# Transposing the heads' outputs by VectorE blocks and moves between partition quarters, instead of by TensorE

## The chip, the core and the metric

The kernel runs on one core of a Trainium2 chip. The metric is the device time of one execution in microseconds, as the median of several runs. A core has TensorE (PE, the matmuls, with its weight loads as PEld), VectorE (DVE), ScalarE (ACT), GpSimd (POOL), SyncE (SP, which here only issues DMAs) and 16 DMA engines. A tile lies in 128 partitions; a "quarter" is 32 of them. TensorE's output goes to PSUM banks of 512 fp32 per partition and is read from there by ACT or DVE ("evicted").

## The reference

One decoder block, 512 tokens, model width 1024, everything fp32. Two branches share the projections of the normed input, a gated short convolution and a four-head mLSTM (256 wide in q and k, 512 in v):

```python
hn = rmsnorm(x, g_mix[l])
proj = jnp.einsum('bsd,de->bse', hn, w_in[l])
(xa, ba, ca, za, q, k, v, o, zb, ig, fg, ga, gb) = jnp.split(proj, SPLIT_POINTS, axis=-1)
ya = ba * causal_short_conv(ca * xa, conv_w[l], conv_b[l])
ya = jnp.einsum('bsc,cd->bsd', ya * jax.nn.silu(za), w_a_out[l])
...
hb = mlstm_chunkwise(q..., k..., v..., ig, fg)          # per head: decayed scores @ v / max(|n.q|, 1)
hb = rmsnorm(hb, g_head[l].reshape(N_HEADS, DV)).reshape(bsz, s, V_DIM).astype(x.dtype)
yb = jax.nn.sigmoid(o) * hb * jax.nn.silu(zb)
yb = jnp.einsum('bsv,vd->bsd', yb, w_b_out[l])
merged = jax.nn.sigmoid(ga) * ya + jax.nn.sigmoid(gb) * yb
x = x + jnp.einsum('bsd,de->bse', merged, w_o[l])
... # a gated per-layer embedding is added, then a last rmsnorm
```

The edit concerns `yb`: each head leaves it as tokens x values (512 x 512), and the product with `w_b_out` needs values x tokens. `g_head` is a factor per value, so it can be applied before or after the transpose, or later.

## The kernel before, in words

**Products.** Each fp32 matmul is three matmuls of a rounded format (`mm3`, L233 to L235): high x high, low x high, high x low. So every weight is split: ACT writes the high part (`whi`, L180), DVE the rest (`wlo`, L181), in halves of 128x1024, shortly before use. The large projections are Strassen products (`strassen`, L318 to L387): seven products (0 to 6) of two steps each, and the weights' sums that they need are made by accumulating DMAs on POOL's queue (`add_chunk`, L156: a second weight block is added in DRAM-to-SBUF transfers onto `wraw`). Plain weight loads are issued by SP (L148).

**Order.** PE, ACT, DVE and POOL work strictly in the order in which the program writes its instructions. `step` (L223) ends each half product: it calls `tick` (L216), which starts fresh tasks (evictions), then emits one half of a weight split, then one piece of every active generator (heads' scores, transposes, loads). A generator that yields 16 times therefore lasts 16 half products, each 2.7 us or more of TensorE. Within a Strassen product the eviction `v` (`snap`, L346, ACT) reads the bank of product 2; product 3 adds into that same bank, so TensorE waits for `v` there.

**Stages** (us in the profiled execution): head 0's v and o (74 to 112), weighted sum `pv` (to 118), z for heads 0 and 1 (to 157), merge gates (to 196), head 1's v and o (to 239), pv (to 246), head 2's q and k (to 288), v and o (to 330), pv (to 337), z for heads 2 and 3 (to 375), gates (to 415), head 3's v and o (to 458), pv (to 465), the convolution's four Strassen products (465 to 628), the convolution's output product (to 666), then `w_b_out`.

**Heads.** `head` fills `vv` (v, high and low; ACT L929, DVE L932) and the normed, gated output `y` (tile `gty`). `turn` (L799) then transposes it: 8 groups of 8 PE transposes of 128x128 (L810), 16 evictions by ACT that apply `g_head` (`gh`, L805) into `yc`, and one DMA of 1 MB on POOL's queue to `yt_d` in DRAM (L813). It is started two or three ticks after the head. The tiles `vv`, `yc` and `qk_raw` (the next head's q and k, loaded by SP at L825) share one buffer in turn (tag "vv"), as does later one half of the convolution's result `ya` (L410). At 628 us the four `yt_d` are loaded again as `yf`, and `left_first` makes the Strassen sums and splits of them.

Of the kernel before, what the change touches and what calls it, by code (L numbers as in the profile page):

```python
# [22 lines left out]
DV = 512  # L23
# [6 lines left out]
HC = 4  # L30
# [6 lines left out]
def hybrid_block(ctx, tc, x, p, g_mix, w_in, conv_w, conv_b, w_a_out, b_gates, g_head,  # L37
                 w_b_out, w_o, g_ple, w_ple_gate, w_ple, g_final, out):
    nc = tc.nc
    act, dve, pool, pe = nc.scalar, nc.vector, nc.gpsimd, nc.tensor  # L40
# [7 lines left out]
    ps_x = ctx.enter_context(tc.tile_pool(name="ps_x", bufs=4, space=bass.MemoryType.PSUM))  # L48
# [21 lines left out]
    H2 = S // 2  # L70
# [47 lines left out]
    spare = {b12[0]: None}  # L118
# [22 lines left out]
    raws, splits, pieces, active, fresh = {}, {}, deque(), [], []  # L141
# [111 lines left out]
    ident = const.tile([P, P], F32, name="ident")  # L253
# [14 lines left out]
    yt_d = [dram.tile([P, 2, HC, H2], F32, name=f"yt_d{h}") for h in range(NH)]  # L268
# [255 lines left out]
    gh = prm[:, 40:56]  # L524
# [48 lines left out]
    def quarter(q):  # L573
        hi, lo = (u[:, q % HH, :] for u in splits[0][q // HH])
        return hi, lo, raws[0][:, q, :]
# [6 lines left out]
    hi, lo, raw = quarter(0)  # L582
# [59 lines left out]
    for g in range(2):  # L642
        src = wg_raw[:, :, g * NH:(g + 1) * NH]
# [57 lines left out]
    B = nc.vector.STREAM_SQUARE_SIZE  # L701
# [94 lines left out]
        a = POFF[j] + (t - j) * P  # L796
        return u[:, a:a + P]

    def turn(h, y):  # L799

        yc = hp.tile([P, 2, 2, HC, H2], F32, name="yc", tag="vv", align_bytes=256)[:, 0]
        pts = {}
        for i in range(3):
            for v in range(2 * i - 2, 2 * i) if i else ():
                act.activation(yc[:, :, v, :], pts[v].rearrange("p (h s) -> p h s", h=2), AF.Copy,  # L805
                               scale=gh[:, 4 * h + v:4 * h + v + 1])
            for v in range(2 * i, 2 * i + 2) if i < 2 else ():
                pts[v] = ps_x.tile([P, S], F32, name="pty", tag="x")
                for t in range(NT):
                    pe.transpose(pts[v][:, t * P:(t + 1) * P], y[:, t, v * P:(v + 1) * P], ident)  # L810
            if i < 2:
                yield
        nc.gpsimd.dma_start(yt_d[h], yc)  # L813

    def qk_tile():
        both = hp.tile([P, 2, 4, S], F32R, name="qk", tag="qk", align_bytes=256)
        return [both[:, i] for i in range(2)]

    def recut(h, qk):

        for _ in range(7):
            yield
        raw = hp.tile([P, 2, 4, S], F32, name="qk_raw", tag="vv", align_bytes=256)[:, 0]
        for m in range(4):
            nc.sync.dma_start(raw[:, m, :], qk_d[h][:, m, :])  # L825
        yield
        yield
        yield
        qk.extend(qk_tile())
        for m in range(4):  # L830
            cut(qk[0][:, m, :], qk[1][:, m, :], raw[:, m, :])
            if m < 3:
                yield
# [69 lines left out]
    def head(h, qk):  # L903
        vv = []

        def sink_qk(n, t, src):

            fs, ps = slice(2 * (t % 2), 2 * (t % 2) + 2), slice(t // 2 * H2, (t // 2 + 1) * H2)
            src = src.rearrange("p (f s) -> p f s", f=2)
            if n == 1:  # L910
                nc.gpsimd.dma_start(qk_d[h + 1][:, fs, ps], src)
                return
            if not qk:
                qk.extend(qk_tile())
            cut(*[u[:, fs, ps] for u in qk], src)
            yield

        if h == 2:
            strassen(hn_lhs, sink_qk, True)
        pr = [hq2.tile([P, 1280], F32R, name=f"pr{i}", align_bytes=256) for i in range(2)]  # L920
        pp = hq2.tile([P, 1280], F32, name="pp")
        gt = []

        def sink_vo(n, t, src):
            if n == 0:
                if not vv:
                    both = hp.tile([P, 2, NT, DV], F32R, name="vv", tag="vv", align_bytes=256)
                    vv.extend(both[:, i] for i in range(2))
                act.activation(vv[0][:, t, :], src, AF.Copy)  # L929
                if t < 2:  # L930
                    yield
                dve.tensor_tensor(vv[1][:, t, :], src, vv[0][:, t, :].bitcast(F32), ALU.subtract)  # L932
            elif h % 2:
                so = temp("e", "so")
                act.activation(so, src, AF.Sigmoid)
                dve.tensor_tensor(gt[0][:, t, :], gt[0][:, t, :], so, ALU.mult)
            else:
                act.activation(gt[0][:, t, :], src, AF.Sigmoid)
            yield

        def scored():
            both = hp.tile([P, 2, NT, DV], F32, name="gty", tag="qk", align_bytes=256)
            gt.extend(both[:, i] for i in range(2))
            if h % 2:
                nc.gpsimd.dma_start(gt[0], z_d[h])

        active.append(scores(h, qk, pr, pp, scored))
        strassen(hn_lhs, sink_vo)
        gt, y = gt

        def weighted_sum(t, ps):
            dve.tensor_scalar(y[:, t, :], ps, inv[:, t:t + 1], None, ALU.mult)
            junk = temp("e", "junk")
# [24 lines left out]
        def sink_z(n, t, src):  # L978
            sz = temp("e", "sz")
            act.activation(sz, src, AF.Sigmoid)  # L980
            if n == 1:
                dve.tensor_tensor(src, sz, src, ALU.mult)
                nc.gpsimd.dma_start(z_d[h + 1][:, t, :], src)
                yield
                return
            dve.tensor_tensor(sz, sz, src, ALU.mult)
            dve.tensor_tensor(gt[:, t, :], gt[:, t, :], sz, ALU.mult)
            yield
            norm(t)
            yield  # L990

        active.append(rsqrt())
        if h % 2 == 0:
            strassen(hn_lhs, sink_z)
        return y

    def finish(h, y, wait):
        for _ in range(wait):
            yield
        yield from turn(h, y)  # L1000

    hp_ctx, hp = open_pool("heads")
    hq_ctx, hq2 = open_pool("scores")
    load_maxima(0)
    qks = [qk_tile()] + [[] for _ in range(3)]
    for h in range(NH):
        y = head(h, qks[h])
        active.append(finish(h, y, 2 + h % 2))
        if h % 2 == 0:
            active.append(recut(h + 1, qks[h + 1]))  # L1010
            strassen(hn_lhs, sink_gate(h))
    close(hq_ctx)

# [15 lines left out]
    yf = {h: (wbp if h == 3 else yfp).tile([P, 2, HC, H2], F32, name=f"yf{h}", tag=f"yf{h}", align_bytes=256) for h in (0, 2, 1, 3)}  # L1029
# [6 lines left out]
    def left_high(k):  # L1036
# [7 lines left out]
        act.activation(units[k][0], src, AF.Copy, scale=scale)  # L1044
        return lambda: dve.scalar_tensor_tensor(both[:, 1], src, scale, both[:, 0].bitcast(F32), ALU.mult, ALU.subtract)

    def left_first():
        for _ in range(5):
            yield
        for k in range(3):  # L1050
            low = left_high(k)
            yield
            low()
            yield
        for g in range(2):
            (a11, a21), (a12, a22) = ([yf[2 * g + r][:, v] for v in range(2)] for r in range(2))
            dve.tensor_tensor(hsf[g], a22, a21, ALU.subtract)
            yield
            dve.tensor_tensor(a21, a11, a21, ALU.subtract)
            yield  # L1060
            dve.tensor_tensor(a11, hsf[g], a11, ALU.add)
            yield
            if g == 0:
                dve.tensor_tensor(a12, a11, a12, ALU.subtract)
                yield
# [18 lines left out]
    todo = deque((n, t) for n, ts in ((0, (0, 1)), (1, range(NT)), (0, (2, 3))) for t in ts)  # L1084
# [140 lines left out]
    half = [slice(0, CW), slice(CW, D)]  # L1225
# [177 lines left out]
    q = [slice(CW, CW + CW // 2), slice(CW + CW // 2, D)]  # L1403
# [50 lines left out]
```

## Time and profile before

| | before |
|---|---|
| runs, median (lowest to highest) | 845.53 us (845.30 to 846.86) |
| the profiled execution, its span | 847.37 us, 845.6 us |
| PE busy | 834.5 us, 4584 instructions |
| DVE, ACT, POOL busy | 651.0, 495.5, 210.0 us |
| granted clock of PE | 0.998 |
| DMA | 173.89 MB, 206 GB/s over the span |
| `yt_d<-yc` put, 1 MB, x4 | 4.9 us from issue to landing (median) |

"Busy" is the time in which an engine executes. An engine's wait is put down to what ended it. A DMA's "landing" is the time from its issue until its last byte is written. Off the path of the busiest engine a wait costs nothing by itself.

### The profile page before, as it was taken

Reading aid. Unit: us, or ns where it says so; the run is one execution under the profiler, and the core shown is the slowest. Engines: PE = TensorE matmul, PEld = TensorE weight load, DVE = VectorE, ACT = ScalarE, POOL = GpSimd, SP = SyncE. Lnnn points to the kernel's source line nnn. Section 1 sums busy time; section 2 is a strip of 40 time slices with the busy share of each in tenths; the row PEclk is TensorE's granted clock in tenths of the full one; section 3 lists DMA queues with packets and bytes.
Section 4 is the critical chain, followed back from the end, with each engine's and each line's share of the span. In section 5 each row is a group of like instructions: output and inputs, shape, how many; then the busy total and the mean of one; then the engine's idle time right before and its main releaser. Section 6 shows DMA issues by size and latency. Waiting matters only on the chain.

```text
span 845.6 us, 12113 instructions
## 1 busy us (share of the span) xinstructions
PE 834.5 (99%) x4584; PEld 726.7 (86%) x4584; DVE 651.0 (77%) x878; ACT 495.5 (59%) x720; POOL 210.0 (25%) x203
## 2 busy tenths in 40 slices
PE   8999999999999999999999999999999999999996
PEld 7888888887889988888788999999998888888885
DVE  5788767975787677788668779897986677999565
ACT  6467665666865566665776654555453256667543
POOL 5203122203124321220222333433411122131031
PEclk9999999999999999999999999999999999999999
DMA  9748779779978997896898799899989488999402
GB/s 310 269 145 183 159 166 220 194 274 227 252 159 207 244 225 180 199 215 199 258 243 211 156 218 169 194 184 182 181 255 380 101 194 214 284 258 229 187 0 100
DMA packets 103939, 173.89 MB, mean 206 GB/s; under 512 B 5632, under 2 KB 46132, under 8 KB 102600
## 3 DMA queue, kind: packets, MB, share of 16 engines
q0 software_dynamic: 39488, 70.33, 44.6%
q1 hardware_dynamic: 59792, 94.64, 33.7%
q10 hardware_dynamic: 4600, 8.14, 3.1%
q8 instruction: 36, 0.59, 0.3%
q14 instruction: 23, 0.19, 0.1%
HBM read 156.30 MB, written 16.79 MB: 205 GB/s over the span
## 4 chain that ended last, share of the span: by engine, by line
PE 92%; DMA 3%; DVE 2%; issue 1%; ACT 1%; SPq 0%; POOL 0%; POOLq 0%; ACTq 0%; DVEq 0%
PE mm L234 28%; PE mm L235 28%; PE mm L233 28%; PE pv L233 1%; PE pv L235 1%; PE pv L234 1%; DMA wraw<-in_w_ple 1%; DMA wraw<-in_w_b_out 1%; PE pty L810 1%; DMA sg_d<-c 1%; PE sc L235 1%; PE sc L234 1%; PE sc L233 1%; DVE wlo L181 1%; PE ptk L1247 0%
## 5 line engine op out<-in xcount | busy, mean ns | idle before, releaser
L181 DVE TENSOR_TENSOR wlo<-wraw,whi 128x1024 fp32r<-128x1024 f32 x244 | 299.4, 1229 | 104.7 <-ACT whi L180 98.8
L180 ACT ACTIVATE whi<-wraw 128x1024 fp32r<-128x1024 f32 x246 | 257.1, 1054 | 103.8 <-PE mm L235 48.8
L156 POOL DMA_DIRECT2D wraw<-in_w_in x112 | 136.9, 1423 | 335.4 <-DVE wlo L181 207.7
L346 ACT ACTIVATE s<-mm 128x512 f32<-128x512 f32 x84 | 50.2, 597 | 100.2 <-PE mm L235 98.7
L233 PE MATMUL mm<-whi,hs 128*128 128x512 f32 x256 | 99.9, 390 | 0.0
L234 PE MATMUL mm<-wlo,hs 128*128 128x512 f32 x256 | 99.8, 390 | 0.0
L235 PE MATMUL mm<-whi,hs 128*128 128x512 f32 x256 | 99.7, 389 | 0.0
L233 PE MATMUL mm<-hn_hi,whi 128*128 128x256 f32 (+1 forms) x304 | 93.3, 307 | 0.0
L235 PE MATMUL mm<-hn_hi,wlo 128*128 128x256 f32 (+1 forms) x304 | 92.9, 306 | 0.0
L234 PE MATMUL mm<-hn_lo,whi 128*128 128x256 f32 (+1 forms) x304 | 92.8, 305 | 0.0
L233 PE MATMUL mm<-hs,whi 128*128 128x256 f32 x320 | 90.9, 284 | 0.0
L234 PE MATMUL mm<-hs,whi 128*128 128x256 f32 x320 | 90.5, 283 | 0.0
L235 PE MATMUL mm<-hs,wlo 128*128 128x256 f32 x320 | 90.5, 283 | 0.0
L234 PE MATMUL mm<-wlo,hn_hi 128*128 128x512 f32 x192 | 75.3, 392 | 0.4 <-DVE wlo L181 0.2
L233 PE MATMUL mm<-whi,hn_hi 128*128 128x512 f32 x192 | 74.9, 390 | 0.0
L235 PE MATMUL mm<-whi,hn_lo 128*128 128x512 f32 x192 | 74.8, 389 | 0.0
L234 PEld LDWEIGHTS mm<-hs,whi 128*128 128x128 f32 x320 | 61.4, 192 | 0.0
L233 PEld LDWEIGHTS mm<-hs,whi 128*128 128x128 f32 x320 | 61.4, 192 | 0.0
L235 PEld LDWEIGHTS mm<-hs,wlo 128*128 128x128 f32 x320 | 61.4, 192 | 0.0
L235 PEld LDWEIGHTS mm<-hn_hi,wlo 128*128 128x128 f32 x304 | 58.1, 191 | 2.5
L234 PEld LDWEIGHTS mm<-hn_lo,whi 128*128 128x128 f32 x304 | 58.1, 191 | 2.4
L233 PEld LDWEIGHTS mm<-hn_hi,whi 128*128 128x128 f32 x304 | 58.1, 191 | 2.4
(339 smaller groups left out, 1670.2 us busy)
## 6 DMA issues: line engine op xcount, KB each, us to landing
wraw<-in_w_in SPq DMA_DIRECT2D x32, 1024.0 KB, 6.1
wraw<-in_w_in POOLq DMA_DIRECT2D x52, 512.0 KB, 8.5
wraw<-in_w_in SPq DMA_DIRECT2D x48, 512.0 KB, 5.6
wraw<-in_w_in POOLq DMA_DIRECT2D x60, 256.0 KB, 5.7
wraw<-in_w_b_out SPq DMA_DIRECT2D x7, 1024.0 KB, 7.0
wraw<-in_w_b_out POOLq DMA_DIRECT2D x12, 512.0 KB, 7.0
wraw<-in_w_o SPq DMA_DIRECT2D x5, 1024.0 KB, 7.4
yt_d<-yc POOLq DMA_DIRECT2D x4, 1024.0 KB, 4.9
```

What stands on the lines that cost most here:

```text
L156: nc.gpsimd.dma_start(raws[to][:, ks, cs], src[:, ks, :], accum_op=ALU.add)
L180: act.activation(hi, t, AF.Copy)
L181: (e_lo or dve).tensor_tensor(lo, t, hi.bitcast(F32), ALU.subtract)
L233: pe.matmul(ps, lhsT=a[0], rhs=b[0], start=first, stop=False, **kw)
L234: pe.matmul(ps, lhsT=a[0], rhs=b[1], start=False, stop=False, **kw)
L235: pe.matmul(ps, lhsT=a[1], rhs=b[0], start=False, stop=last, **kw)
L346: act.activation(to[i], src, AF.Copy, scale=scale)
L810: pe.transpose(pts[v][:, t * P:(t + 1) * P], y[:, t, v * P:(v + 1) * P], ident)
```

## The change: what it does

- The PE transposes and their evictions go. `turning(h, half)` gives three functions: `turn(y, t)` transposes 32x32 blocks of a 128x512 tile on DVE (one instruction), `move(i, on_dve)` copies one of 16 combinations of a source quarter and a destination quarter (32 partitions) on DVE or ACT, `put(i)` sends a part to `yt_d`.
- Even heads work in two halves of two tiles each (2 x 16 moves of 256 elements, a put of 512 KB after each); odd heads in one go (16 moves of 512 elements, then two puts of 512 KB, in pieces of 1 KB). Heads 0 and 2 give ACT 22 moves and DVE 10, head 1 eight each, head 3 eleven and five.
- The steps are spread over 16 ticks by plans of (ACT moves, DVE moves) per tick, so that the last put of heads 0 and 2 comes in the next odd head's v and o stage, that of head 1 in head 2's, and that of head 3 in the convolution.
- `qk_raw` is no tile of its own: it takes the other half of the even head's `yc`, and is loaded by SP earlier.
- The first two tiles of an even head are transposed one tick after their norm in z's sink; `sink_qk` waits four ticks before its first two cuts.
- `g_head` is applied to the loaded `yf` by 16 ACT operations of 128x512 in `left_first` (`scale_head`).

```diff
-    def turn(h, y):
-        yc = hp.tile([P, 2, 2, HC, H2], F32, name="yc", tag="vv", align_bytes=256)[:, 0]
...
-                act.activation(yc[:, :, v, :], pts[v].rearrange("p (h s) -> p h s", h=2), AF.Copy,
-                               scale=gh[:, 4 * h + v:4 * h + v + 1])
...
-                    pe.transpose(pts[v][:, t * P:(t + 1) * P], y[:, t, v * P:(v + 1) * P], ident)
...
-        nc.gpsimd.dma_start(yt_d[h], yc)
+    def turning(h, half):
+        both = hp.tile([P, 2, NT, DV], F32, name="yc", tag="vv", align_bytes=256)
+        spare, blocks, spread = both[:, 0], both[:, 0], both[:, 1].rearrange("p t v -> p (t v)")
+        n = NT
+        if half:
+            n = NT // 2
+            blocks, spread = both[:, 1, :n], both[:, 1, n:].rearrange("p t v -> p (t v)")
+        spread = spread.rearrange("p (v s) -> p v s", v=HC)
+        def turn(y, t):
+            dve.transpose(blocks[:, t % n, :], y[:, t, :])
+        def move(i, on_dve):
+            b, q = divmod(i, P // B)
+            src = blocks[b * B:(b + 1) * B].rearrange("p t (v q a) -> p t v q a", q=P // B, a=B)[:, :, :, q]
+            dst = spread[q * B:(q + 1) * B].rearrange("p v (t b a) -> p t v b a", t=n, a=B)[:, :, :, b]
+            if on_dve:
+                dve.tensor_copy(dst, src)
+            else:
+                act.activation(dst, src, AF.Copy)
+        def put(i):
+            nc.gpsimd.dma_start(yt_d[h][:, i], spread if half else spread[:, :, i * H2:(i + 1) * H2])
...
+    def finish(h, y, tools):
+        turn, move, put, _ = tools or turning(h, False)
+        if h % 2 == 0:
+            yield from moves(move, [(2, 0), (2, 0), (3, 0), (3, 0), (2, 0), (1, 0), (2, 0), (1, 0)])
+            put(0)
+            for t in (2, 3):
+                turn(y, t)
                 yield
+            yield from moves(move, [(0, 1), (0, 1), (1, 3), (1, 1), (2, 2), (2, 2)])
+            put(1)
+            return
+        for _ in range(4):
+            yield
+        for ts in ((0,), (1,), (2,), (3,)) if h == 1 else ((0, 1), (), (2,), (3,)):
+            for t in ts:
+                turn(y, t)
+            yield
+        yield from moves(move, [(1, 1)] * 8 if h == 1 else [(3, 0), (3, 1), (2, 1), (1, 1), (2, 2)])
+        for i in range(2):
+            put(i)
...
-        raw = hp.tile([P, 2, 4, S], F32, name="qk_raw", tag="vv", align_bytes=256)[:, 0]
...
+            for _ in range(4 if t < 2 else 0):
+                yield
...
+    def scale_head(h):
+        for v in range(HC):
+            act.activation(yf[h][:, :, v, :], yf[h][:, :, v, :], AF.Copy, scale=gh[:, HC * h + v:HC * h + v + 1])
     def left_first():
         for _ in range(5):
             yield
+        for h in (0, 2):
+            scale_head(h)
+            yield
         for k in range(3):
             low = left_high(k)
             yield
             low()
-            yield
+            if k:
+                scale_head(2 * k - 1)
+                yield
```

Three places in the order of instructions follow. A row is line, operation, output<-input and the output's shape; in brackets are the semaphores that it waits for: an engine's name stands for that engine, DMASW for the landing of a DMA issued by POOL, DMAHW for one issued by SP or ACT.

POOL, from the end of head 0's gate stage into head 1's v and o stage, before (`wraw` are the accumulating weight loads, `yt_d` the put of the head's output):

```order
L983 DMA z_d_100<-c 128x512 [waits DVE_49]
L813 DMA yt_d_90<-yc 128x2048 [waits DMASW1_49,Activation_49]
L156 DMA wraw_1609<-in_w_in 128x2x512 [waits DMAHW4_49,DMAHW7_49,DMASW2_49,DVE_49]
L156 DMA wraw_1609<-in_w_in 128x2x512 [waits DMASW3_49,DVE_49]
L156 DMA wraw_1692<-in_w_in 128x2x512 [waits DMAHW1_49,DMAHW0_49,DMASW4_49]
L156 DMA wraw_1692<-in_w_in 128x2x512 [waits DMASW5_49]
L156 DMA wraw_1609<-in_w_in 128x2x512 [waits DMASW6_49,DMASW2_49,DVE_49]
L156 DMA wraw_1609<-in_w_in 128x2x512 [waits DMASW7_49,DMASW3_49,DVE_49]
```

The same place now:

```order
L822 DMA yt_d_90<-yc 128x1024 [waits DMASW1_49,Activation_49]
L156 DMA wraw_1598<-in_w_in 128x2x512 [waits DMAHW3_49,DMAHW7_49,DMASW2_49,DVE_49]
L156 DMA wraw_1598<-in_w_in 128x2x512 [waits DMASW3_49,DVE_49]
L156 DMA wraw_1686<-in_w_in 128x2x512 [waits DMAHW4_49,DMAHW1_49,DMASW4_49]
L156 DMA wraw_1686<-in_w_in 128x2x512 [waits DMASW5_49]
L156 DMA wraw_1598<-in_w_in 128x2x512 [waits DMASW6_49,DMASW2_49,DVE_49]
L822 DMA yt_d_90<-yc 128x1024 [waits DMASW7_49]
L156 DMA wraw_1598<-in_w_in 128x2x512 [waits DMASW3_49,DMASW0_49,DVE_49]
```

The put of 2048 elements ahead of all the loads is now two of 1024, and the second stands behind the fifth load.

ACT, in the first half of head 1's v and o stage, before (`e` are the exponentials of the scores, `vv` the new head's v, `v` the Strassen eviction, `whi` the weight split):

```order
L872 ACTIVATE e<-mxb,colsb 128x128 x2
L929 ACTIVATE vv<-c 128x512 [waits DMASW1_49]
L346 ACTIVATE v<-mm 128x512 [waits PE_49]
L180 ACTIVATE whi_1943<-wraw_1739 128x1024 [waits Activation_49]
L872 ACTIVATE e<-mxd,colsb 128x128 [waits DVE_49,Activation_49]
```

Now:

```order
L916 ACTIVATE e<-mxb,colsb 128x128 x2
L975 ACTIVATE vv<-c 128x512 [waits DMASW7_49,Activation_49]
L346 ACTIVATE v<-mm 128x512 [waits PE_49]
L180 ACTIVATE whi_1955<-wraw_1735 128x1024
L916 ACTIVATE e<-mxd,colsb 128x128 [waits DVE_49,Activation_49]
```

The order around it is the same; `vv` waited for the landing of the one put (DMASW1), and now waits for that of the second put (DMASW7) and for the moves.

DVE, about 45 us into the convolution, before and then now (`ya` is the convolution's result, in the buffer that held head 3's `yc`):

```order
L410 TENSOR_TENSOR ya_4712<-cv,ya_4711 128x2x256 [waits DMASW4_49]
L447 TENSOR_TENSOR m<-m,cz 128x512
L181 TENSOR_TENSOR wlo_4778<-wraw_4434,whi_4777 128x1024 [waits Activation_49]
L399 TENSOR_SCALAR cv<-cu,prm 128x256 [waits DVE_49]
L401 SCALAR_TENSOR_TENSOR cv<-cu,prm,cv 128x256 [waits DVE_49] x2
```

```order
L181 TENSOR_TENSOR wlo_4722<-wraw_4292,whi_4721 128x1024 [waits PE_49,Activation_49]
L445 TENSOR_TENSOR m<-c 128x512 [waits DVE_49]
L455 COPY cu<-cu 128x2x2
L456 TENSOR_TENSOR cu<-m,mm 128x2x256 [waits DVE_49,PE_49]
L181 TENSOR_TENSOR wlo_4763<-wraw_4435,whi_4762 128x1024 [waits DMAHW2_49,DMAHW1_49,Activation_49]
L410 TENSOR_TENSOR ya_4730<-cv,ya_4729 128x2x256 [waits DMASW7_49,DMASW0_49]
L447 TENSOR_TENSOR m<-m,cz 128x512
L181 TENSOR_TENSOR wlo_4796<-wraw_4435,whi_4795 128x1024 [waits Activation_49]
```

`ya` waited for one put, and now for both of head 3's; a weight split stands right behind it. On POOL these two puts stand behind the first four 256 KB loads of `wraw_4292` (weights of the convolution).

More of the change, by code (lines that the diff above doesn't have):

```diff
@@ L797, in ptile @@
         return u[:, a:a + P]
-    def turn(h, y):
-        yc = hp.tile([P, 2, 2, HC, H2], F32, name="yc", tag="vv", align_bytes=256)[:, 0]
[L802 to L805, printed above, removed]
-                               scale=gh[:, 4 * h + v:4 * h + v + 1])
[L807 to L811, printed above, removed]
-                yield
-        nc.gpsimd.dma_start(yt_d[h], yc)
+    def turning(h, half):
[18 more added lines that the diff above has]
+            nc.gpsimd.dma_start(yt_d[h][:, i], spread if half else spread[:, :, i * H2:(i + 1) * H2])
+        return turn, move, put, spare
@@ new lines, in moves @@
+    def moves(move, plan):
+        todo = deque(range((P // B) ** 2))
+        for n_act, n_dve in plan:
+            for i in range(max(n_act, n_dve)):
+                if i < n_act:
+                    move(todo.popleft(), False)
+                if i < n_dve:
+                    move(todo.popleft(), True)
+            yield
+        assert not todo
+    def finish(h, y, tools):
[5 more added lines that the diff above has]
+                turn(y, t)
+                yield
+            yield from moves(move, [(0, 1), (0, 1), (1, 3), (1, 1), (2, 2), (2, 2)])
[10 more added lines that the diff above has]
+            put(i)
@@ L817, in qk_tile, with recut @@
         return [both[:, i] for i in range(2)]
-    def recut(h, qk):
+    def recut(h, raw, qk):
         for _ in range(7):
             yield
-        raw = hp.tile([P, 2, 4, S], F32, name="qk_raw", tag="vv", align_bytes=256)[:, 0]
         for m in range(4):
@@ L990, in sink_z @@
             yield
+            if t < 2:
+                yield
+                if not tools:
+                    tools.extend(turning(h, True))
+                tools[0](y, t)
+                yield
+        tools = []
         active.append(rsqrt())
@@ L994, in head @@
             strassen(hn_lhs, sink_z)
-        return y
-    def finish(h, y, wait):
-        for _ in range(wait):
-            yield
-        yield from turn(h, y)
+        return y, tools
     hp_ctx, hp = open_pool("heads")
@@ L1006, in hybrid_block @@
     for h in range(NH):
-        y = head(h, qks[h])
-        active.append(finish(h, y, 2 + h % 2))
+        y, tools = head(h, qks[h])
+        active.append(finish(h, y, tools))
         if h % 2 == 0:
-            active.append(recut(h + 1, qks[h + 1]))
+            active.append(recut(h + 1, tools[3], qks[h + 1]))
             strassen(hn_lhs, sink_gate(h))
@@ L1045, in left_high @@
         return lambda: dve.scalar_tensor_tensor(both[:, 1], src, scale, both[:, 0].bitcast(F32), ALU.mult, ALU.subtract)
+    def scale_head(h):
+        for v in range(HC):
+            act.activation(yf[h][:, :, v, :], yf[h][:, :, v, :], AF.Copy, scale=gh[:, HC * h + v:HC * h + v + 1])
     def left_first():
         for _ in range(5):
+            yield
+        for h in (0, 2):
+            scale_head(h)
             yield
@@ L1053, in left_first @@
             low()
-            yield
+            if k:
+                scale_head(2 * k - 1)
+                yield
         for g in range(2):
```

## The prediction

> **What bounds the kernel now.** I read the page's busy times and its chain first, then the groups of the tile that the change removes, then the stages by windows, the waits, and last the timeline at the places where the order of instructions changes.
>
> ```profile
> PE 834.5 (99%) x4584; PEld 726.7 (86%) x4584; DVE 651.0 (77%) x878; ACT 495.5 (59%) x720; POOL 210.0 (25%) x203
> PE 92%; DMA 3%; DVE 2%; issue 1%; ACT 1%; SPq 0%; POOL 0%; POOLq 0%; ACTq 0%; DVEq 0%
> ```
>
> TensorE is busy for 834.5 of 845.6 us and is 92% of the chain that ended last. So the time is a stream of matmuls with hardly a hole in it: whatever leaves TensorE is gained in full, whatever runs on another engine is free until a matmul has to wait for it, and from there on it costs in full.
>
> ```profile
> L810 PE MATMUL pty<-ident,gty x64: 270/272/273, 164.7 to 480.8; 128*128 128x128 f32 x64
> L805 ACT ACTIVATE yc<-pty,prm x16: 672/682/692, 166.5 to 482.3; 128x512 f32<-128x512 f32 x16
> ...
> 164.90 0.87 PE pty L810 x8
> ```
>
> The 64 transposes are 8 groups of 8. A group holds the chain of waits for 0.87 us.
>
> **The change: what it removes.** 8 groups × 0.87 us = 7.0 us leave TensorE, all of it on the path, since nothing else fills TensorE's time there. The 16 evictions on ScalarE (16 × 0.68 = 10.9 us) ran beside matmuls; their loss is worth nothing by itself.
>
> **What it adds on VectorE and ScalarE.** No row of this profile shows a move between partition quarters of this size, so I take bounds.
>
> ```profile
> L891 DVE STREAM_TRANSPOSE pp<-pp 128x512 f32<-128x512 f32 x4 | 2.8, 706 | 0.0
> L895 DVE COPY pp<-pp 32x16 f32<-32x16 f32 x12 | 2.0, 164 | 0.2
> L399 DVE TENSOR_SCALAR cv<-cu,prm 128x256 f32<-128x256 f32 x16 | 6.2, 385 | 0.0
> ...
> L240 ACT ACTIVATE qk<-qk_raw 128x512 fp32r<-128x512 f32 x8 | 4.9, 619 | 0.0
> L875 ACT ACTIVATE pr<-pp 128x256 fp32r<-128x256 f32 x4 | 1.6, 410 | 0.7 <-DVE pp L880 0.6
> ```
>
> A block transpose is 16 × 0.71 = 11.3 us in all. A move of 256 elements is between 0.16 (the small copy L895) and 0.39 us (L399) on VectorE, and I take 0.39, since L399 has its length; on ScalarE 0.41 (L875). A move of 512 is taken at 0.7 on VectorE (as L891, the same length) and 0.62 on ScalarE (L240). Heads 0 and 2: 22 moves on ScalarE = 9.0 us and 10 on VectorE = 3.9 us each. Head 1: 8 × 0.62 = 5.0 and 8 × 0.7 = 5.6. Head 3: 11 × 0.62 = 6.8 and 5 × 0.7 = 3.5. The 16 g_head scalings (128x512, 0.62) are 9.9 us of ScalarE. VectorE gains 28 us, ScalarE 29 net of the evictions. What counts is where.
>
> ```profile
> 185.80:200.70 14.90, 14.81 (x64) 11.66 (x63) 9.62 (x13) 12.48 (x20) 3.13 (x4) 1.00 0.80 246
> 196.00:239.00 43.00, 42.91 (x194) 34.94 (x193) 31.36 (x51) 31.05 (x48) 10.29 (x9) 1.00 1.02 249
> 628.00:666.00 38.00, 38.00 (x169) 31.43 (x169) 25.54 (x33) 11.36 (x12) 6.04 (x10) 1.00 0.83 302
> ```
>
> The columns are the stretch, its length, then busy us of PE, PEld, DVE, ACT and POOL, the granted clock, the DMA share and GB/s. The scalings fall in 628 to 666, where ScalarE is busy 11.4 of 38 us: 9.9 more fit, cost 0; without that cover each would delay a weight split by 0.6. The tight place is the end of a gate stage (185.8 to 200.7): ScalarE has 2.4 us free, and the moves of the even head sit between the splits there. About 0.9 us per even head would reach TensorE (two or three VectorE moves of 0.39 ahead of one wlo); but the next stall, below, is pinned to a DMA that started before, and takes this delay in. I count 0 for it, and up to 2 × 0.9 = 1.8 as a bound. Transposes and the other moves fit beside: VectorE has 43.0 − 31.4 = 11.6 us free in 196 to 239.
>
> **The moved puts: the term that decides.** Before, each head's output left as one 1 MB put (L813) shortly after the head, long ahead of its buffer's next use. Now the last put of a head stands 16 or 17 ticks later, in the next odd stage for heads 0 and 2. In POOL's order it comes right behind the fifth accumulating weight load (L156, `wraw`) of that stage. The tile `vv` of the next head takes the same buffer, so ScalarE's first `vv` (L929, L975 in the new kernel) waits for the put's landing. Behind it in ScalarE's queue stands the eviction `v` (L346), which empties the bank that the fourth Strassen product adds into; TensorE waits for that, and for the half operand split (`whi`, L180, `wlo`, L181) behind it.
>
> How long do these loads take to land? First the four loads of 197.1 to 200.3, then the fifth:
>
> ```profile
> L156 POOL DMA_DIRECT2D wraw<-in_w_in x4: 1227/1465/2199, 197.1 to 200.3; - x4
> ...
> DMA to landing us min/median/max: 7.7/10.9/14.9
> L156 POOL DMA_DIRECT2D wraw<-in_w_in x1: 1194/1194/1194, 207.5 to 207.5; - x1
> ...
> DMA to landing us min/median/max: 11.2/11.2/11.2
> ```
>
> The first lands at 204.8, the fourth at 200.3 + 14.9 = 215.2, the fifth at 207.5 + 11.2 = 218.7: one 512 KB load each 3.5 us, in the order of issue (the five take 13.9 us from the first landing to the last), with a DMA share of 1.02 in this stage. So a put issued behind the fifth cannot overtake it. What it takes beyond is shown by a plain 1 MB transfer behind such a load:
>
> ```profile
> gty<-z_d POOLq DMA_DIRECT2D x1, 1024.0 KB, 7.7
> wraw<-in_w_in POOLq DMA_DIRECT2D x1, 512.0 KB, 6.0
> ```
>
> The load was issued at 224.2 and landed at 230.2, gty at 225.1 and 232.8: 2.6 us later for 1 MB, so 1.3 us for a 512 KB put.
>
> The row of issues and landings says: strictly in order. [...] Were the put free of the loads ahead, the waits below would be near 0 and the sum a gain (the first rival). The trace goes against it in every one of these landings.
>
> Stall A (head 0's put, head 1's vv):
>
> ```profile
> 214.36 0.62 ACT L929 ACTIVATE vv<-c 128x512 fp32r<-128x512 f32 x1
> 214.88 0.58 ACT L346 ACTIVATE v<-mm 128x512 f32<-128x512 f32 x1
> 215.36 1.05 ACT L180 ACTIVATE whi<-wraw 128x1024 fp32r<-128x1024 f32 x1
> ...
> 216.44 1.23 DVE L181 TENSOR_TENSOR wlo<-wraw,whi 128x1024 fp32r<-128x1024 f32 x1 [1.00 <-ACT whi L180]
> 216.62 0.40 PE L233 MATMUL mm<-whi,hs 128*128 128x512 f32 x1
> ```
>
> The put lands at 218.7 + 1.3 = 220.0; vv and v then end at about 221.05 (0.52 from start to start, 0.58 for v). TensorE wanted the bank at 216.62: 4.4 us. Then whi and wlo end at 223.3, against 221.05 + 6 matmuls of 0.23 = 222.4 when the second half is wanted: 0.9 more. A = 5.3 us.
>
> Stalls B (head 1's two puts, head 2's vv) and C (head 2's, head 3's):
>
> ```profile
> L156 POOL DMA_DIRECT2D wraw<-in_w_in x1: 1197/1197/1197, 297.0 to 297.0; - x1
> ...
> DMA to landing us min/median/max: 10.3/10.3/10.3
> 302.16 0.62 ACT L929 ACTIVATE vv<-c 128x512 fp32r<-128x512 f32 x1
> 307.76 0.40 PE L233 MATMUL mm<-whi,hs 128*128 128x512 f32 x1
> L156 POOL DMA_DIRECT2D wraw<-in_w_in x1: 1194/1194/1194, 426.2 to 426.2; - x1
> ...
> DMA to landing us min/median/max: 10.3/10.3/10.3
> 432.24 0.62 ACT L929 ACTIVATE vv<-c 128x512 fp32r<-128x512 f32 x1
> 435.50 0.40 PE L233 MATMUL mm<-whi,hs 128*128 128x512 f32 x1
> ```
>
> B: the load lands at 307.3, both puts at 307.3 + 2.6 = 309.9, vv and v end at 311.0, wanted 307.76: 3.3 + 0.9 for the split = 4.2 us. C: 436.5 + 1.3 = 437.8, v ends at 438.9, wanted 435.50: 3.4 + 0.9 = 4.3 us.
>
> Stall D: `ya` of the convolution (L410 on VectorE) takes the buffer of head 3's output and now waits for both of its puts, which stand behind four 256 KB loads.
>
> ```profile
> L156 POOL DMA_DIRECT2D wraw<-in_w_in x4: 1194/1444/1703, 504.5 to 508.0; - x4
> ...
> DMA to landing us min/median/max: 4.4/5.6/6.2
> 509.51 0.68 DVE L410 TENSOR_TENSOR ya<-cv,ya 128x512 fp32r<-128x512 f32 x1
> ...
> 511.58 1.23 DVE L181 TENSOR_TENSOR wlo<-wraw,whi 128x1024 fp32r<-128x1024 f32 x1 [0.78 <-ACT whi L180]
> 513.58 0.28 PE L235 MATMUL mm<-hn_hi,wlo 128*128 128x256 f32 x1
> ```
>
> The last load lands at 508.0 + 6.2 = 514.2, the puts at 516.8; ya, the op of the same shape behind it and wlo then end at 516.8 + 0.6 + 0.6 + 1.2 = 519.2 to 519.7 (0.5 for the puts' smaller pieces), against 513.58 when TensorE reads that wlo: D = 6.1 us at the upper end, which I take, since two puts of 1 KB pieces are shown by no row.
>
> **The sum.** −7.0 + 5.3 + 4.2 + 4.3 + 6.1 = +12.9 us. The profiled execution took 847.37 us (span 845.6 and 1.8 around it); 847.4 + 12.9 = 860.3. The median of the runs is 845.53, 1.8 below the profiled one, so the forecast for a median is 858 us. The rest of the change (a head's scores load issued earlier by SP, its cut four ticks later, the scalings) I count as 0, with spare time of a tick or more behind each.
>
> **Rivals.**
> - The puts are hidden (the other side). The mechanism: each last put lands before its buffer is wanted, either because its packets pass the accumulating loads or because those land earlier. For it: a put alone is quick (4.7 to 5.1 us for 1 MB, below) and POOL would issue it at 208.7 (207.5 + 1.2), 5.7 us before vv. Against it: all landings above are in order. It decides if the put lands by the time vv's slack is used up, 216.62 − 1.1 = 215.5 in A, 3.2 us before the load ahead of it did. Then −7.0 + 1.8 (gate) = −5.2: 840 us.
>
> ```profile
> L813 POOL DMA_DIRECT2D yt_d<-yc x4: 545/572/602, 170.5 to 483.3; - x4
> ...
> DMA to landing us min/median/max: 4.7/4.9/5.1
> ```
>
> - The puts are hidden, but the moves overload ScalarE at the end of the gate stages: five moves come there, and at 1.1 us each (as a 128x1024 split) instead of 0.41 they need 5.5 us where 2.4 are free, 3.1 us lost per even head, 6.2 against 7.0 gained: 845 us, no change. For it: the window row; against it: a 256-element move is shorter than any 128x1024 op of ScalarE.
> - Two of the four waits are smaller. The gate-to-vo boundary has a wait of its own, which a different timing of the DMAs may shift:
>
> ```profile
> DVE c L350 <- DMA sg_d<-c: 5.8, 2, 3.0
> ```
>
>  With the loads of A and C landing 2 to 3 us earlier, these two fall to about 2.5 each and the time to 853 us; with D at half as well, 850.
> - The puts are worse than 1.3 us each: the pieces are smaller, and every later load of the stage is pushed back by the same amount, so that a `whi` waits again. Twice 1.3 us more at each of the four places would be +10: 868 us.
>
> **How the numbers follow.** The forecast as summed, 854 to 863 us: 0.55. Smaller waits, 848 to 854: 0.18. Worse puts, over 863: 0.15, two thirds of it below 867. Puts hidden: 0.07. Overload alone: 0.05. A measurement of this kernel tells about 0.2% (1.7 us) from no change. So faster 0.08, same 0.05, slower 0.87. The range, 849 to 866, leaves out the two hidden cases and the far tail.
>
> **What would show it.** No pty on PE, and PE busy near 827.5 us. In the waits of ScalarE, vv (L975) on the put's DMA, 3 times, 5.5 to 8 us each; in VectorE's, ya (L410) on the same, about 7 us; TensorE's idle before the fourth product of three vo stages, 4 to 5 us each. STREAM_TRANSPOSE at 0.7 us ×16 at L810; ScalarE moves at 0.4 to 0.62; the scalings beside a full TensorE. I would be wrong if the puts' landings show them ahead of the loads issued before them, if vv does not wait, or if a move takes twice its price and the gate stages stretch.

## The result, and the profile after

| | before | after |
|---|---|---|
| median of the runs | 845.65 us | 865.89 us (864.66 to 867.66) |
| ratio, 95% interval | | 1.0238 (1.0217 to 1.0260) |
| the profiled execution, its span | 847.37, 845.6 us | 864.66, 862.8 us |
| granted clock of PE | 0.998 | 0.989 |

The kernel is 20.2 us slower. The profiled executions differ by 17.3 us (that of before was its slowest run, that of after its fastest); the sums on traces below are made against these 17.3.

The page, engines and chain:

```profile
PE 834.4 (97%) x4520; PEld 723.8 (84%) x4520; DVE 672.1 (78%) x927; ACT 528.6 (61%) x783; POOL 213.7 (25%) x207
PE 79%; DMA 6%; ACT 6%; DVE 4%; issue 3%; POOL 1%; ACTq 0%; SPq 0%; POOLq 0%; DVEq 0%
PE mm L235 24%; PE mm L234 24%; PE mm L233 24%; DMA yt_d<-yc 5%; ACT whi L180 2%; DVE wlo L181 2%; PE pv L234 1%; PE pv L233 1%; PE pv L235 1%; DMA gty<-z_d 1%; ACT yc L819 1%; DMA xin<-in_x 1%; POOL wraw L156 1%; ACT qk L240 1%; ACT c L781 0%
```

The 64 transposes are gone (4520 instructions instead of 4584), and the landing of the puts `yt_d` is now 5% of the chain. But look at PE's busy time: 834.4 us against 834.5. Seven microseconds of transposes left, and the busy time stayed. The matmuls that remain are booked with 7 us more. The other 17.3 us are idle: 862.8 − 834.4 = 28.4 against 845.6 − 834.5 = 11.1. So the books of the profiled runs are −7.0 (transposes) + 17.3 (idle) + 6.9 (busy time added to the matmuls that remain) = +17.2.

The waits of TensorE, ScalarE and VectorE (total, times, longest):

```profile
PE mm L233 <- ACT v L346: 8.2, 3, 3.9
PE mm L235 <- DVE wlo L181: 6.4, 1, 6.4
PE mm L234 <- DVE wlo L181: 3.9, 6, 0.9
ACT vv L975 <- DMA yt_d<-yc: 19.4, 3, 8.3
DVE ya L410 <- DMA yt_d<-yc: 7.5, 1, 7.5
```

Three waits for `v` are the stalls A, B and C (2.15, 3.9 and 2.15 us), the one of 6.4 is D, and of the six short ones four (0.48, 0.76, 0.75 and 0.76 us, 2.75 in all) lie where a gate stage passes into a v and o stage, two (0.32 and 0.87) further on. The cause is in the fourth and fifth row: `vv` three times and `ya` once wait for a put.

Where the put lands, at A: the fifth accumulating load, and the put behind it on POOL's queue.

```profile
L156 POOL DMA_DIRECT2D wraw<-in_w_in x1: 1194/1194/1194, 206.3 to 206.3; - x1
...
DMA to landing us min/median/max: 9.3/9.3/9.3
L822 POOL DMA_DIRECT2D yt_d<-yc x1: 1061/1061/1061, 207.1 to 207.1; - x1
...
DMA to landing us min/median/max: 10.1/10.1/10.1
```

The load lands at 215.7, the put at 217.2, 1.5 us behind it. At C the put takes 10.2 us and lands 1.7 us behind its load, at B the two puts take 11.4 and 11.8 us.

Why the matmuls are slower: the stretch behind stall A, by windows (columns as in the prediction; the granted clock, which follows POOL's busy time, is the share of full speed that TensorE is given).

```profile
215.00:217.00 2.00, 1.30 (x9) 1.01 (x7) 0.00 (x0) 0.00 (x0) 0.00 (x0) 1.00 1.09 305
217.00:219.00 2.00, 0.56 (x2) 0.48 (x3) 0.00 (x0) 1.72 (x3) 0.00 (x0) 1.00 0.86 160
219.00:221.00 2.00, 2.00 (x6) 1.59 (x5) 1.63 (x3) 2.00 (x6) 0.00 (x0) 0.52 0.06 12
221.00:223.00 2.00, 2.00 (x7) 1.53 (x6) 1.24 (x3) 2.00 (x5) 0.00 (x0) 0.63 0.57 132
223.00:225.00 2.00, 2.00 (x14) 1.75 (x13) 2.00 (x4) 1.43 (x3) 1.05 (x1) 1.00 1.11 386
```

TensorE resumes at 218.4, and from 219.0 to 222.4 the clock granted is 0.51: a matmul every 0.43 us instead of every 0.23. Eight of them cost 1.6 us, and they are booked as busy. The same follows B (1.7 us) and D (1.4); behind B:

```profile
314.00:316.00 2.00, 2.00 (x7) 1.25 (x7) 1.57 (x2) 2.00 (x6) 0.00 (x0) 0.66 0.01 2
316.00:318.00 2.00, 2.00 (x5) 1.53 (x5) 1.24 (x3) 2.00 (x5) 0.00 (x0) 0.50 0.57 140
```

Behind C the clock stays at 1.00:

```profile
446.00:448.00 2.00, 1.69 (x8) 1.07 (x7) 2.00 (x3) 2.00 (x6) 0.00 (x0) 1.00 0.02 5
```

So the clock accounts for 4.7 of the 6.9 us. The other 2.2 come from how busy time is counted around a wait, by an estimate from the timeline: a matmul of 128x512 is shown 0.39 us long, but the next starts 0.23 us later; ahead of a wait 0.16 us of the last one is no longer overlapped, and the first one behind it holds TensorE for 0.34 instead of 0.23. That is 0.27 us of busy time for each wait, and eight waits were added.

### The profile page after: what moved, and what is told of

Its sections match the earlier page's. It is cut to its first block, busy times and chain, and to the rows that moved or that the text cites. A ratio compares the mean times of both kernels' runs of the same rounds, so it can differ in the third digit from the quotient of the medians.

```text
span 862.8 us, 12094 instructions
## 1 busy us (share of the span) xinstructions
PE 834.4 (97%) x4520; PEld 723.8 (84%) x4520; DVE 672.1 (78%) x927; ACT 528.6 (61%) x783; POOL 213.7 (25%) x207
## 4 chain that ended last, share of the span: by engine, by line
PE 79%; DMA 6%; ACT 6%; DVE 4%; issue 3%; POOL 1%; ACTq 0%; SPq 0%; POOLq 0%; DVEq 0%
PE mm L235 24%; PE mm L234 24%; PE mm L233 24%; DMA yt_d<-yc 5%; ACT whi L180 2%; DVE wlo L181 2%; PE pv L234 1%; PE pv L233 1%; PE pv L235 1%; DMA gty<-z_d 1%; ACT yc L819 1%; DMA xin<-in_x 1%; POOL wraw L156 1%; ACT qk L240 1%; ACT c L781 0%
## 5 line engine op out<-in xcount | busy, mean ns | idle before, releaser
L233 PE MATMUL mm<-whi,hs 128*128 128x512 f32 x256 | 101.2, 395 | 8.2 <-ACT v L346 8.2
L234 PE MATMUL mm<-wlo,hs 128*128 128x512 f32 x256 | 101.2, 395 | 0.3 <-DVE wlo L181 0.3
L235 PE MATMUL mm<-whi,hs 128*128 128x512 f32 x256 | 101.1, 395 | 0.0
L234 PE MATMUL mm<-hn_lo,whi 128*128 128x256 f32 (+1 forms) x304 | 93.4, 307 | 0.0
L234 PE MATMUL mm<-hs,whi 128*128 128x256 f32 x320 | 90.6, 283 | 0.0
L234 PE MATMUL mm<-wlo,hn_hi 128*128 128x512 f32 x192 | 75.5, 393 | 3.6 <-DVE wlo L181 3.6
L233 PEld LDWEIGHTS mm<-whi,hs 128*128 128x128 f32 x256 | 48.7, 190 | 18.7 <-ACT v L346 8.8
L234 PEld LDWEIGHTS mm<-hs,whi 128*128 128x128 f32 x320 | 61.5, 192 | 0.0
```

What stands on the lines that cost most here:

```text
L233: pe.matmul(ps, lhsT=a[0], rhs=b[0], start=first, stop=False, **kw)
L234: pe.matmul(ps, lhsT=a[0], rhs=b[1], start=False, stop=False, **kw)
L235: pe.matmul(ps, lhsT=a[1], rhs=b[0], start=False, stop=last, **kw)
```

## The experiments

Each is compared with the kernel before, run on the same chip (845.7 to 846.0 us). The changed kernel was not run again beside them: where a difference from it is given, its time is the 865.89 us above, beside which the kernel before took 845.65.

**1. All puts on ScalarE's queue.**

```diff
-            nc.gpsimd.dma_start(yt_d[h][:, i], ...)
+            nc.scalar.dma_start(yt_d[h][:, i], ...)
```

> All eight puts of the heads' outputs are issued by ScalarE, on its hardware queue, at the same ticks; nothing else is changed. Theory (the puts wait behind the accumulating loads of POOL's queue, the next vv and ya wait for them, and TensorE then restarts at half clock): a 512 KB put takes 4 to 7 us on its own queue, issued near 206.5, so it lands before vv is due at 214; the waits of vv (19.4 us) and ya (7.5 us) fall under 3 us together, the granted clock returns to 0.998, and the time is 845.7 - 7 (transposes) + 2 to 4 (small stalls of the gate stages, which stay) = 841 to 843 us. Rival (the moves overload ScalarE and VectorE, the puts only show it): the time stays at 858 or above, since the moves are all there. Rival (any put so late lands late, whatever its queue, because the DMA engines are full in these stages): the waits stay, 862 to 868.

Measured: 854.55 us, ratio 1.0098 (1.0078 to 1.0119). The expected 841 to 843 was missed. The stalls A and C are gone and D is 0.9 us, but B is longer than in the changed kernel (7.5 us instead of 3.9): the puts of head 1 take 14 to 19 us, so there the second rival came true.

```profile
PE mm L233 <- ACT v L346: 7.5, 1, 7.5
PE mm L234 <- DVE wlo L181: 3.5, 5, 1.0
...
L822 ACTq DMA_DIRECT2D yt_d<-yc x2: 377/651/925, 292.4 to 292.8; - x2
...
  ACT vv L975: 11.6, 1
...
DMA to landing us min/median/max: 14.4/16.8/19.1
```

So POOL's queue was the cause at A, C and D (11 of 20 us gone with the moves untouched, against the rival on the moves), and something else makes the puts of head 1 slow. Experiments 5 and 7 take that up.

**2. Only head 3's puts on ScalarE's queue.**

```diff
-            nc.gpsimd.dma_start(yt_d[h][:, i], ...)
+            (nc.scalar if h == 3 else nc.gpsimd).dma_start(yt_d[h][:, i], ...)
```

> Only head 3's two puts go to ScalarE's queue; those of heads 0 to 2 stay on POOL's. Theory with the clock: of the changed kernel's 865.9 us the stall of ya goes, 6.5 us of idle and 1.4 to 1.8 us of slow matmuls behind it: 865.9 - 8 = 857 to 859 us. Without a clock term only the idle goes: 859.5 us; under the rival that the moves cost, less than 3 us go.

Measured: 857.86 us, ratio 1.0150 (1.0133 to 1.0167), 8.0 us below the changed kernel. `ya` waits 2.0 us instead of 7.5, and TensorE's idle there falls from 6.4 to 0.9. The idle alone is 5.5; the slow restart behind it (1.4 us) is gone too, by the granted clock of the two kernels behind that place (0.50 in the changed one, 1.00 here):

```profile
530.00:532.00 2.00, 1.95 (x9) 1.95 (x10) 1.93 (x4) 0.00 (x0) 0.00 (x0) 0.50 0.34 79
```

```profile
524.00:526.00 2.00, 2.00 (x19) 2.00 (x18) 1.97 (x4) 0.96 (x1) 0.34 (x1) 1.00 1.01 292
```

The remaining 1.1 us of the 8.0 is within what single runs of the changed kernel differ by (864.7 to 867.7).

**3. The transposes of before, with the late puts.** The puts of `turn` are delayed to the ticks of the changed kernel, and `qk_raw` takes the other half of `yc`:

```diff
-        nc.gpsimd.dma_start(yt_d[h], yc)
+        for i in range(2):
+            for _ in range((4, 8)[i] if h % 2 == 0 else ((11, 0) if h == 1 else (8, 0))[i]):
+                yield
+            nc.gpsimd.dma_start(yt_d[h][:, i], yc[:, i])
```

> The kernel before, with its TensorE transposes and evictions, but the output is put in two halves of 512 KB at the ticks of the changed kernel (the second half of heads 0 and 2 behind the fifth accumulating load, both halves of heads 1 and 3 likewise); the next head's q and k take the other half of the tile, as in the changed kernel. No block transposes, no moves. Theory: the same four waits and slow restarts as in the changed kernel, without its small gate stalls and without the gain of 7 us: 845.7 + 2 to 3 (A), 5.7 (B), 3 (C), 8 (D) and up to 3 of variation = 864 to 870 us. Rival (the moves cost): 845 to 848 us.

Measured: 870.35 us, ratio 1.0292 (1.0277 to 1.0308). With no block transpose and no move, the late puts cost 24.4 us.

```profile
PE mm L233 <- ACT v L346: 12.0, 3, 4.4
PE mm L235 <- DVE wlo L181: 6.5, 1, 6.5
```

The same four waits; the three for `v` add up to 12.0 us instead of 8.2. The accumulating loads ahead were issued later there (the first of head 1's stage at 194.7 us instead of 193.1). The short waits of L234 for `wlo` do not occur at all, so in the changed kernel they come with the transposes and moves on VectorE and ScalarE.

**4. Matmuls of no use in two of the stalls.**

```diff
+                if j == 3 and fill:
+                    idle = ps_x.tile([P, S], F32, name="idle", tag="x")
+                    for _ in range(fill):
+                        pe.matmul(idle, lhsT=x[0][:, 0, :P], rhs=w[0][0], start=True, stop=True)
-        strassen(hn_lhs, sink_vo)
+        strassen(hn_lhs, sink_vo, fill=(0, 9, 17, 0)[h])
```

> The changed kernel with matmuls of no use (128x128 by 128x512, into a spare bank, their result is read by nobody) put on TensorE ahead of the fourth Strassen product of head 1's (9 of them, 2.0 us) and head 2's (17, 3.9 us) v and o stages, where it sits idle for 2.15 and 3.9 us. Theory of the clock: TensorE never falls idle there, so the matmuls behind run at 0.23 instead of 0.43 us: 1.6 and 1.75 us less, 865.9 - 3.3 = 861.5 to 863.5 us, and the nine slow matmuls behind each of the two places are gone from the trace. Rival (the matmuls behind are slow because of their operands or their bank): they stay slow, and the time is 866 or, where a stall is shorter than its filler, a little above.

Measured: 861.96 us, ratio 1.0189 (1.0174 to 1.0205): 3.9 us less than the changed kernel, by adding 26 matmuls. The windows behind stall A, with the filler:

```profile
217.00:219.00 2.00, 2.00 (x10) 1.60 (x9) 0.28 (x1) 2.00 (x5) 0.00 (x0) 1.00 0.68 124
219.00:221.00 2.00, 1.69 (x8) 1.08 (x7) 2.00 (x3) 2.00 (x5) 0.00 (x0) 1.00 0.02 7
221.00:223.00 2.00, 2.00 (x13) 1.75 (x12) 1.24 (x3) 2.00 (x4) 0.00 (x0) 1.00 0.96 281
```

The clock stays at 1.00, where the changed kernel had 0.52 and 0.63. Behind B, where 17 of them fill the stall, it stays at 1.00 as well. So the slow matmuls are due to the idle time ahead of them, not to their operands or bank. The slow stretch behind A lasted 3.4 us (219.0 to 222.4) in the changed kernel. A gap of 2.15 us was enough for it there, while one of 2.15 at C was not; what decides between the two is not shown.

**5 and 6. The odd heads' transposes and moves sooner**, once with all puts on ScalarE's queue, once with all on POOL's:

```diff
-        for _ in range(4):
+        for _ in range(2):
             yield
-        for ts in ((0,), (1,), (2,), (3,)) if h == 1 else ((0, 1), (), (2,), (3,)):
+        for ts in ((0,), (1,), (2,), (3,)):
...
-        yield from moves(move, [(1, 1)] * 8 if h == 1 else [(3, 0), (3, 1), (2, 1), (1, 1), (2, 2)])
+        yield from moves(move, [(2, 2)] * 4 if h == 1 else [(3, 0), (3, 1), (2, 1), (1, 1), (2, 2)])
```

> All puts on ScalarE's queue, and the transposes and moves of heads 1 and 3 sooner: they begin two ticks after the head instead of four, and head 1's 16 moves take four ticks (two on ScalarE and two on VectorE each) instead of eight. So head 1's puts are issued about 6 ticks (17 us) and head 3's 2 ticks sooner, before the full v and o stage begins. Theory: head 1's puts, which on ScalarE's queue took 14 to 19 us in that stage and made vv wait 11.6 us, land before 295; the 7.5 us stall and the 2.2 us of slow restart behind it vanish, head 3's 0.9 too: 854.5 - 9.7 - 0.9 = 843 to 845 us. Rival (the moves cost as much wherever they are, doubled up per tick they cost more): 850 us or above.

Measured: 843.41 us, ratio 0.9971 (0.9962 to 0.9981): faster than before. Head 1's puts, issued at 276.8, still take 10.4 and 14.3 us, but land at about 291, ahead of `vv`. What TensorE still waits for:

```profile
PE mm L234 <- DVE wlo L181: 2.7, 5, 0.8
```

> The same sooner transposes and moves of heads 1 and 3, with all puts left on POOL's queue as in the changed kernel; heads 0 and 2 as there. Theory: the stalls before head 2 (5.7 us with its slow restart) and of ya (8 us) go, since these puts are issued before the loads of the full stages; those of heads 0 and 2 stay: 865.9 - 13.7 = 851 to 854 us. Rival (the queue is the cause, not the time): 863 or above.

Measured: 851.70 us, ratio 1.0071 (1.0056 to 1.0086), 14.2 us below the changed kernel. So the time of the put decides as well as its queue: on the same queue, issued before the full stage, the puts of heads 1 and 3 make TensorE wait no more. A and C remain (1.72 and 1.88 us of idle in two waits for `v`), and the clock stays at 1.00 behind both.

**7. Larger pieces.** Puts on ScalarE's queue at the late ticks; the odd heads' two puts of 1 KB pieces become one of 8 KB pieces, and the reload of `yf` undoes the layout.

```diff
+            if half:
+                nc.scalar.dma_start(yt_d[h][:, i], spread)
+            elif i:
+                nc.scalar.dma_start(yt_d[h].rearrange("p i v s -> p (i v s)"), spread.rearrange("p v s -> p (v s)"))
```

> All puts on ScalarE's queue at the late ticks, but heads 1 and 3 write their output in one put of 1 MB whose pieces are 8 KB instead of 1 KB (the layout in DRAM differs, and the load of yf reads it in 1 KB pieces). If the puts of head 1 took 14 to 19 us because a queue gets a turn per packet and its packets are small, the 1 MB now lands in 6 to 9 us, near 300: vv waits under 2 us and the time is 854.5 - 7 to 9.7 = 845 to 848 us. If the DMA engines are simply full (share 1.1), it lands as late and the time stays at 853 to 856 us.

Measured: 844.35 us, ratio 0.9980 (0.9970 to 0.9989). The put issued at 292.4, as in experiment 1, now lands after 9.1 us with twice the bytes (of the two puts of this line the shortest is head 3's, the longest head 1's; the second row is ScalarE's wait):

```profile
DMA to landing us min/median/max: 4.7/6.9/9.1
ACT vv L978 <- DMA yt_d<-yc: 1.4, 3, 1.0
```

That is a little below the expected 845 to 848. In the same full stage and on the same queue, 1 MB took 19.1 us in two puts of 1 KB pieces and 9.1 in one of 8 KB; whether one put instead of two has a part in it was not tried by itself. From 292 to 304 us that queue moved 0.45 MB in 443 packets in experiment 1, and 1.05 MB in 144 packets here: 1.0 KB a packet against 7.3. That a queue gets a turn per packet, the condition in the expectation, was the author's assumption; no run shows the turns.

**8. g_head alone.** The kernel before, with unscaled evictions and `scale_head` in `left_first`.

> The kernel before, with g_head taken out of the evictions and applied by 16 ScalarE operations to the loaded outputs, as in the changed kernel; nothing else. By every theory here this is hidden beside TensorE: 845 to 847 us, no difference that can be told. Rival (they delay the first weight splits of w_b_out's product): up to 16 x 0.62 = 10 us more.

Measured: 845.92 us, ratio 1.0000 (0.9991 to 1.0009). ScalarE's busy time in the stretch from 628 to 666 rises from 11.4 to 20.9 us, and TensorE stays full:

```profile
628.00:666.00 38.00, 38.00 (x169) 31.44 (x168) 24.44 (x32) 20.91 (x28) 6.18 (x10) 1.00 0.84 302
```

**9. The even heads' last 16 moves all on VectorE** (added to experiment 5):

```diff
-            yield from moves(move, [(0, 1), (0, 1), (1, 3), (1, 1), (2, 2), (2, 2)])
+            yield from moves(move, [(0, 1), (0, 1), (0, 2), (0, 2), (0, 5), (0, 5)])
```

> As early_odd_act (843.4 us), and the second half's 16 moves of heads 0 and 2 all on VectorE, one or two a tick while ScalarE cuts the next head's q and k, five in each of the last two ticks. Their short moves take 0.28 us there against 0.41 on ScalarE, which has no free moment from 190 to 205. Theory: of the 3.5 to 4 us that TensorE still loses at the ends of the two gate stages, the part behind the six ScalarE moves goes: 1.2 us per head, 843.4 - 2.4 = 840.5 to 842 us. Rival (VectorE becomes the late engine there): 843 to 846.

Measured: 843.59 us, ratio 0.9968 (0.9958 to 0.9978), the same as experiment 5. The profiled run (span 841.8) shows 2.0 us of waits for wlo instead of 2.7; the medians show nothing. The expected 2.4 us did not come. The time lies in the rival's range (VectorE late), but with fewer waits for wlo the trace does not bear that rival out.

**10. All of it**: experiment 9 with the 8 KB pieces, and the first 16 moves of the even heads as `[(2, 0), (3, 0), (3, 0), (2, 0), (1, 0), (1, 1), (1, 1), (1, 0)]`.

> As late_moves_dve, with the 8 KB pieces of the odd heads' puts and with the first half's moves spread so that fewer fall in the ticks where ScalarE was late at 170 us (two of them on VectorE). Theory: the same, less the 0.4 us stall at 170: 840 to 842 us. Rival (the reload of yf in 1 KB pieces, or the sooner first moves, cost): 843 or above.

Measured: 843.04 us, ratio 0.9964 (0.9950 to 0.9977). The expected 840 to 842 was missed, and its interval overlaps those of 5 and 9. It beats both kernels, by 2.9 and 22.8 us, with TensorE's own waits down to

```profile
PE mm L234 <- DVE wlo L181: 1.4, 2, 0.8
```

TensorE's busy time is 828.0 us, 6.5 below the 834.5 of before. Of the 7.0 us that the transposes held, 2.9 are kept in the medians. The profiled spans differ by 5.4 (845.6 to 840.2), but there the profiled run of before was slower than the four other runs of its session (845.3 to 846.9), and that of this kernel the fastest of its five. What takes the rest in the medians stays open.

## Why the prediction was right, and where it was off

The direction, the four places and what makes TensorE wait there were right. That the time lies in the range is partly luck: the median of 865.89 is 0.1 us under its end of 866, two of the four runs are above it, and the sum was 7.9 us too small (858). It also lies outside the 854 to 863 that got 0.55, in the branch of the worse puts (0.15), whose cause did not occur.

- **The transposes, −7.0.** Right for TensorE: it has no pty, its busy time is 6.5 us lower in experiment 10, and with the waits removed (experiments 5, 7, 10) the kernel is faster than before, though by 1.3 to 2.9 us only.
- **Strictly in order of issue, 1.3 us per put.** Right: 1.5 at A, 1.3 to 1.7 elsewhere. Moving the puts off that queue (1, all but B) or ahead of the loads (6, B and D) removes the waits; putting late without any moves (3) makes them.
- **A 5.3 and C 4.3: idle of 2.15 each.** Too large. At A the loads ahead landed 3 us sooner (the fifth at 215.7 instead of 218.7), as the third rival had it: the wait of VectorE for `sg_d` (5.8 us in 2 waits, before) is gone, and the first load of the stage was issued 4 us sooner (193.1 instead of 197.1), in both kernels 0.3 us behind the end of a `wlo` that VectorE does after that place. That the one follows from the other is likely, not shown: the profile of before names a DMA as what ended POOL's wait. The store `sg_d` in question took 6.5 us to land before (issued at 188.4) and 3.3 now (at 186.6); why was not tried by itself. Of the 0.9 us for the split behind the stall, 0.32 came at C, and at A the slow clock covered it.
- **B 4.2: 3.9. D 6.1: 6.4.** Right, though B is 3.9 of waiting for `v` alone, where the sum had 3.3 and 0.9 for the split.
- **Slow matmuls behind a stall: not in the sum at all, 4.7 us in the profiled run (of 6.9 of added busy time).** This is the step that failed. The prediction took a stall as idle time alone. Experiment 4 shows that at A and B the idle time also costs 1.6 to 1.7 us behind it.
- **The gate stages, counted 0, bound 1.8.** Too small: four waits of 2.75 us, 3.9 with the two further on. Experiment 3, without moves, has none of them, and experiment 5, without any of the long stalls, keeps 2.7. "The next stall takes this delay in" was argued from a DMA that started before. The chain that ended last shows something else ahead of the put of A:

```profile
203.72 1.07 ACT whi L180
204.81 1.24 DVE wlo L181
207.06 10.13 DMA yt_d<-yc
```

 POOL issues the fifth load when that `wlo` has ended (at 206.3), and the put behind it; ahead of this `whi` ScalarE has six moves of 0.41 us from 191.5 on. So by this chain the delay is handed on to the put and not taken in; how much of the landing hangs on the issue, and how much on the loads ahead, is not shown.
- **Durations of the moves.** ScalarE 0.41 and 0.62 us against 0.41 and 0.63 measured; VectorE 0.39 and 0.70 against 0.31 and 0.45 (rows below). The scalings are 0.71 instead of 0.62, and hidden as said (8).

```profile
L819 ACT ACTIVATE yc<-yc 32x256 f32<-32x256 f32 x44 | 18.2, 414 | 0.8
L819 ACT ACTIVATE yc<-yc 32x512 f32<-32x512 f32 x19 | 12.0, 630 | 1.2 <-DVE yc L810 0.8
L1097 ACT ACTIVATE yf<-yf,prm 128x512 f32<-128x512 f32 x16 | 10.1, 707 | 0.0
...
L817 DVE COPY yc<-yc 32x256 f32<-32x256 f32 x20 | 6.2, 311 | 0.4
L817 DVE COPY yc<-yc 32x512 f32<-32x512 f32 x13 | 5.9, 451 | 0.4
```

So two errors (A and C too large by 5.3; the short waits, the clock and the busy time counted around each wait, all at 0 in the sum, about 11) partly cancelled. In the profiled runs the sum is 4.4 us short (12.9 against 17.3); most of the rest of the 7.9 comes from the profiled run of before being its slowest and that of after its fastest. Of the rivals, "hidden puts" did not occur, and of "overload" only the 2.75 us above, with moves at 0.41 us and not at 1.1; the third came half true, for A and C; the fourth, worse puts on POOL's queue, did not, and the time came out near its figure (868) because of the clock and the short waits.

## What to carry to other kernels

Before work is moved off the bounding engine, look at what the last step of the moved work releases: here a store of head 0 that had 39 us to spare was put behind accumulating loads on one queue, and the next users of such buffers were ready 5 us or less after the last put was issued (4.4 at A, 0 at D). Issue such a store on another queue, and there before the busy stage or in large pieces. And price a stall of the matmul engine at its idle time plus the slow restart, which in the changed kernel was 1.4 to 1.7 us for three stalls of 2 to 6 us and nothing for the fourth.

## What the runs showed of the hardware that was not expected

- A gap of 2.15 us between matmuls (A) was followed by 3.4 us at a granted clock of 0.51 (219.0 to 222.4); the other gap of the same length (C) was not. Over the changed kernel and experiments 1 to 4 and 6, none of the five stalls of 1.7 to 2.0 us was followed by a lower clock, and all nine of 3.6 to 7.5 us were (0.50 in the changed kernel behind 3.9 and 6.4). The mean granted clock of the profiled executions goes with it: 0.997 in experiment 6, which has two of the five and none of the nine, and 0.987 in experiment 3, which has four of the nine.
- On ScalarE's queue beside accumulating loads, 1 MB in two puts of 1 KB pieces took 19.1 us to land, in one put of 8 KB pieces 9.1.
- A copy of 32 partitions between quarters takes as long on ScalarE as an operation on 128 partitions of the same length (0.41 us for 256 elements, L819 and L875); VectorE does it in 0.31.
